# Accumulating weight transfers ordered behind two sums on POOL's queue in a Strassen-style FFN

## The chip, the cores and the metric

The kernel runs on 1 core of one Trainium2 chip. The metric is the device time of one execution in microseconds (us), the median of several runs. The core has five engines that run unsynchronized except for semaphores: PE (matrix multiply), DVE (vector), ACT (activations and copies), POOL (general purpose, and the issuer of transfers that add to their destination) and SP (issuer of plain transfers).

## The reference

Two layers of a decoder trunk over 512 tokens of width 1024, float32. Each layer is four blocks, and the first and the last are gated feed-forward blocks (FFN), so the program holds four of them:

```python
def swiglu(x, w_in, w_out):
    a, b = jnp.split(x @ w_in, 2, axis=-1)
    return (jax.nn.silu(a) * b) @ w_out

for l in range(DEPTH):   # DEPTH = 2; D_MODEL = 1024, D_FF = 2816
    x = layer_norm(ALPHA * x + 0.5 * swiglu(x, ffn1_w_in[l], ffn1_w_out[l]), ...)
    x = layer_norm(ALPHA * x + hybrid_mixer(x, ...), ...)
    x = layer_norm(ALPHA * x + cross_attention(x, mem, ...), ...)
    x = layer_norm(ALPHA * x + 0.5 * swiglu(x, ffn2_w_in[l], ffn2_w_out[l]), ...)
```

## The kernel before, in words

**Arithmetic.** Every float32 operand of a matmul is kept as two rounded parts, high (H) and low (L). A product is three matmuls: `wH` with `xTH`, `wH` with `xTL`, `wL` with `xTH` (printed in this order in the profile as `xTH,wH`, `xTL,wH`, `xTH,wL`). `prep` makes the parts of a weight tile `raw`: ACT copies to `wH`, then DVE writes `wL = raw - wH`. With `share` DVE does only half of `wL` and POOL the other half. The activations x^T lie in `xTH` and `xTL`.

**First half of an FFN.** The columns of `w_in` are worked in 22 column groups of 128 for the gate (part 0) and for the linear factor (part 1). The first four groups (`PLAIN = 2` pairs, f = 0 to 3) are plain products. Groups f = 0, 1 have their first 256 tokens computed while the block before still finishes (`early`, matmuls 256 wide), then their last 256 tokens, and f = 2, 3 run over all 512 tokens (matmuls 512 wide). In the second FFN of layer 0 the four weights of f = 2, 3 are the tiles numbered 7585 (f = 2, part 0), 7616 (f = 2, part 1), 7649 (f = 3, part 0) and 7680 (f = 3, part 1), as `wH`; their `wL` have the next number (7586, 7617, 7650, 7681), and the PSUM banks they fill are 7589, 7620, 7653 and 7684.

The other 9 pairs (q = 2 to 10) use a Strassen-Winograd scheme: 2x2 blocks, seven products instead of eight. It needs four sums and differences of blocks of x^T (T1 to T4) once per FFN, and for each q sums and differences of weight blocks.

**The T's (`combine`).** Four tiles `xr` are xTH + xTL of the four blocks of x^T: POOL makes B11 and B21 (both of the first 256 tokens, `xr_7512` and `xr_7518` in the second FFN), DVE makes B12 and B22 (`xr_7514`, `xr_7516`). DVE then takes differences one from the other, beginning with `xr_7512 <- xr_7514 - xr_7512`, which needs POOL's first sum, and each difference is split into H and L by a copy on ACT and a subtraction on DVE (tiles `T`).

**The weight sum S1.** For each q a tile `sw` is loaded with a plain transfer from SP's queue, and two transfers from POOL's queue then add the second block to it while they write (`accum_op=ALU.add`, two slices of 256 KB each). POOL's queue holds two tiles' worth ahead (`bufs=2`), so two of these pairs stand in POOL's order near the start of an FFN.

**What sets the order.** Nothing in the code fixes POOL's order in general. A scheduler places each engine's instructions by priority and by its own estimate of when operands are ready; each engine then runs its list strictly in that order, and waits at an instruction until its semaphores are reached. `add_manual_dep` with `NoSync` adds an edge that the scheduler must respect, without a semaphore. In the first FFN (program start) the scheduler put POOL's two `xr` sums ahead of the accumulating transfers; in the other three it put two pairs of transfers (four instructions) ahead of the sums.

## Time and profile before

| | us |
|---|---|
| median of 3 runs | 2257.73 (2257.27 to 2258.74) |
| the profiled execution's own time | 2261.62 |
| its span in the trace | 2259.9 |
| PE busy in that span | 2199.5 |
| DVE / ACT / POOL busy | 1449.6 / 928.7 / 287.4 |
| time of PE without an instruction, put down to DVE's `wL` | 38.6, in 8 waits |

Times in the rows are microseconds from the span's start. A timeline row gives the start, the duration, engine, line, operation, `out<-in` without buffer numbers, shapes and count (several like instructions can be merged into one row), and in brackets the engine's idle time before it and the work that ended it. A row of waits gives the waiter, what it waited for, the total, the number of times and the longest.

### The profile page before, as it was taken

What the parts mean: (1) busy time and instruction counts of PE and PEld (TensorE: products, weight loads), DVE (VectorE), ACT (ScalarE), POOL (GpSimd) and SP (SyncE); (2) the same over time, 40 slices, a digit from 0 to 9 for tenths busy, and PEclk for the clock granted to TensorE, in tenths of its full rate; (3) what the DMA queues carried; (4) which work ended last, traced back from release to release, by engine and by line L of the source; (5) the groups of instructions that cost most, each with busy time, mean ns of one, the idle gap of its engine ahead of it and who ended that gap; (6) DMA issues with size and microseconds to landing.
All of it is one profiled execution on the core that took longest, in us unless ns stands there. A gap on an engine that the chain in (4) does not pass through costs nothing.

```text
span 2259.9 us, 33859 instructions
## 1 busy us (share of the span) xinstructions
PE 2199.5 (97%) x13952; PEld 1980.9 (88%) x13952; DVE 1449.6 (64%) x2016; ACT 928.7 (41%) x1405; POOL 287.4 (13%) x336
## 2 busy tenths in 40 slices
PE   9999999999999989999979999999999999899998
PEld 8999888888788879998869998888887988799987
DVE  6677636777675667773457776367776755777734
ACT  4444512467433234461224454134674332344511
POOL 3110001340010211100121100014300102111000
PEclk9999999999999989999989999999999999899999
DMA  8565433223331446643265554232233215456431
GB/s 227 158 166 150 140 103 96 77 86 112 100 112 56 140 112 159 168 150 103 78 170 149 143 147 136 88 114 74 73 112 112 94 56 145 122 145 167 150 103 47
DMA packets 238143, 273.62 MB, mean 121 GB/s; under 512 B 8058, under 2 KB 196762, under 8 KB 237988
## 3 DMA queue, kind: packets, MB, share of 16 engines
q1 hardware_dynamic: 218404, 252.58, 35.1%
q0 software_dynamic: 19584, 18.88, 5.6%
q8 instruction: 109, 1.79, 0.3%
q14 instruction: 46, 0.38, 0.1%
HBM read 267.76 MB, written 3.67 MB: 120 GB/s over the span
## 4 chain that ended last, share of the span: by engine, by line
PE 83%; DVE 8%; issue 4%; POOL 2%; DMA 1%; ACT 1%; SPq 0%; DVEq 0%; POOLq 0%; ACTq 0%
PE ps L194 81%; DVE wL L121 2%; PE ps L199 2%; DVE x_nat L121 1%; DVE xTL L121 1%; DVE st L121 1%; DMA sw<-in_ffn_w_in_dram 1%; POOL mlrs L121 1%; POOL sw L121 1%; DVE xr L121 0%; DVE T L121 0%; POOL xr L121 0%; DVE Cb L121 0%; DMA x_nat<-in_x_dram 0%; DMA raw<-in_ffn_w_in_dram 0%
## 5 line engine op out<-in xcount | busy, mean ns | idle before, releaser
L121 DVE TENSOR_TENSOR wL<-raw,wH 128x1024 fp32r<-128x1024 f32 (+2 forms) x423 | 504.8, 1195 | 488.9 <-ACT wH L121 484.9
L121 ACT CAST wH<-raw 128x1024 fp32r<-128x1024 f32 (+2 forms) x423 | 439.9, 1044 | 767.7 <-PE ps L194 572.7
L194 PE MATMUL ps<-xTH,wL 128*128 128x256 f32 (+1 forms) x1712 | 525.1, 307 | 38.1 <-DVE wL L121 38.1
L194 PE MATMUL ps<-xTH,wH 128*128 128x256 f32 (+1 forms) x1712 | 527.5, 309 | 1.0 <-ACT sc L121 1.0
L194 PE MATMUL ps<-xTL,wH 128*128 128x256 f32 (+1 forms) x1712 | 525.1, 307 | 2.9 <-DVE xTL L121 2.9
L194 PE MATMUL ps<-T,wH 128*128 128x256 f32 x2304 | 418.6, 283 | 0.0
L194 PEld LDWEIGHTS ps<-xTH,wL 128*128 128x128 f32 x1712 | 330.0, 193 | 55.2 <-DVE wL L121 40.8
L194 PEld LDWEIGHTS ps<-T,wH 128*128 128x128 f32 x2304 | 359.4, 192 | 0.5
L194 PEld LDWEIGHTS ps<-xTL,wH 128*128 128x128 f32 x1712 | 330.2, 193 | 17.9 <-DVE xTL L121 5.3
L194 PEld LDWEIGHTS ps<-xTH,wH 128*128 128x128 f32 x1712 | 329.9, 193 | 14.5 <-ACT sc L121 1.2
L194 PE MATMUL ps<-T,wL 128*128 128x256 f32 x1152 | 326.3, 283 | 0.5 <-DVE wL L121 0.5
L194 PE MATMUL ps<-wH,hH 128*128 128x512 f32 x704 | 274.6, 390 | 0.0
L194 PE MATMUL ps<-wH,hL 128*128 128x512 f32 x704 | 274.5, 390 | 0.0
L194 PE MATMUL ps<-wL,hH 128*128 128x512 f32 x704 | 274.1, 389 | 0.0
L194 PEld LDWEIGHTS ps<-T,wL 128*128 128x128 f32 x1152 | 221.2, 192 | 0.9 <-DVE wL L121 0.7
L121 POOL DMA_DIRECT2D sw<-in_ffn_w_in_dram x72 | 87.7, 1219 | 627.0 <-issue 245.9
L121 POOL TENSOR_TENSOR rs<-ve,mhalf 128x1 f32<-128x1 f32 x32 | 29.8, 931 | 1079.0 <-DVE ve L121 1079.0
L194 PEld LDWEIGHTS ps<-wH,hL 128*128 128x128 f32 x704 | 132.1, 188 | 28.4 <-DVE hL L121 1.3
L194 PEld LDWEIGHTS ps<-wL,hH 128*128 128x128 f32 x704 | 132.2, 188 | 27.3
L194 PEld LDWEIGHTS ps<-wH,hH 128*128 128x128 f32 x704 | 132.2, 188 | 27.2
L121 ACT CAST wH<-sw 128x1024 fp32r<-128x1024 f32 x72 | 75.5, 1048 | 130.9 <-DVE sw L121 90.7
L121 DVE TENSOR_TENSOR wL<-sw,wH 128x1024 fp32r<-128x1024 f32 x72 | 87.9, 1221 | 22.6 <-ACT wH L121 22.5
(243 smaller groups left out, 2964.6 us busy)
## 6 DMA issues: line engine op xcount, KB each, us to landing
raw<-in_ffn_w_in_dram SPq DMA_DIRECT2D x147, 512.0 KB, 6.2
raw<-in_ffn_w_out_dram SPq DMA_DIRECT2D x40, 1024.0 KB, 5.0
raw<-in_ffn_w_in_dram SPq DMA_DIRECT2D x28, 1024.0 KB, 7.1
sw<-in_ffn_w_in_dram SPq DMA_DIRECT2D x36, 512.0 KB, 3.5
sw<-in_ffn_w_in_dram POOLq DMA_DIRECT2D x72, 256.0 KB, 4.6
raw<-in_xattn_w_kv_dram SPq DMA_DIRECT2D x16, 1024.0 KB, 5.6
raw<-in_mix_w_in_dram SPq DMA_DIRECT2D x18, 512.0 KB, 4.0
raw<-in_mix_w_in_dram SPq DMA_DIRECT2D x8, 1024.0 KB, 5.2
```

Of the source, the lines that this page charges most:

```text
L121: return f(*a, **k)
L194: self.nc.tensor.matmul(out, l, r, start=start, stop=stop, **k)
L199: self.nc.tensor.transpose(out, i, ident)
```

## The change

The transfers that add to `sw` get an edge behind POOL's second sum (`self.summed`, the last instruction that the loop over the four sums made, which is B21 on POOL). The edge is order alone, on one engine; no wait is added. The helper that made such edges for `behind` is split out as `order`.

```diff
     def behind(self, ins, i):
 
         if self.hold is not None:
-            self.tc.add_manual_dep(ins.ins, self.hold[i].ins.name, mybir.DependencyInfo(
-                mybir.DependencyClass.NoSync, mybir.DependencyReason.DATA), reason="order")
+            self.order(ins, self.hold[i])
+
+    def order(self, ins, before):
+        self.tc.add_manual_dep(ins.ins, before.ins.name, mybir.DependencyInfo(
+            mybir.DependencyClass.NoSync, mybir.DependencyReason.DATA), reason="order")
...
         for e, x in ((G, "B11"), (V, "B12"), (V, "B22"), (G, "B21")):
             H, L = self.right(x)
             r[x] = self.two("xr").rearrange("p a (k n) -> p (a k) n", k=2)
-            e.tensor_add(r[x], H.bitcast(F32), L.bitcast(F32))
+            i = e.tensor_add(r[x], H.bitcast(F32), L.bitcast(F32))
+        self.summed = i
...
             for k in (0, 2):
-                nc.gpsimd.dma_start(s[:, k:k + 2], self.block(q, 1, 1)[:, k:k + 2], accum_op=ALU.add)
+                i = nc.gpsimd.dma_start(s[:, k:k + 2], self.block(q, 1, 1)[:, k:k + 2], accum_op=ALU.add)
+
+                n.order(i, self.summed)
```

The number of instructions on each engine is the same. The order differs at one place of the second, third and fourth FFN, and there in the same way; the first FFN keeps its order.

POOL, at the start of the second FFN's transfers (`sw_7717` and `sw_7882` are the S1 tiles of q = 2 and q = 3):

```order
 L121 TENSOR_TENSOR wL_7416<-raw_7413,wH_7415 128x512
+L121 TENSOR_TENSOR xr_7512<-xTH_7114,xTL_7115 128x1024
+L121 TENSOR_TENSOR xr_7518<-xTH_7114,xTL_7115 128x1024
 L121 DMA sw_7717<-in_ffn_w_in_dram 128x2x256 x2
 L121 DMA sw_7882<-in_ffn_w_in_dram 128x2x256 x2
-L121 TENSOR_TENSOR xr_7512<-xTH_7114,xTL_7115 128x1024
-L121 TENSOR_TENSOR xr_7518<-xTH_7114,xTL_7115 128x1024
 L121 DMA sw_8107<-in_ffn_w_in_dram 128x2x256 x2
```

The two sums moved up past four accumulating transfers. DVE, at the same place (`h_7461` is the gated hidden tile of f = 0, multiplied by its second factor in bank 7342):

```order
+L121 TENSOR_TENSOR xr_7514<-xTH_7114,xTL_7115 128x1024
+L121 TENSOR_TENSOR xr_7516<-xTH_7114,xTL_7115 128x1024
+L121 TENSOR_TENSOR h_7461<-h_7461,ps_7342 128x512
+L121 TENSOR_TENSOR xr_7512<-xr_7514,xr_7512 128x1024
 L121 TENSOR_TENSOR wL_7586<-raw_7583,wH_7585 128x1024
-L121 TENSOR_TENSOR xr_7514<-xTH_7114,xTL_7115 128x1024
-L121 TENSOR_TENSOR h_7461<-h_7461,ps_7342 128x512
-L121 TENSOR_TENSOR xr_7516<-xTH_7114,xTL_7115 128x1024
-L121 TENSOR_TENSOR xr_7512<-xr_7514,xr_7512 128x1024
-L121 TENSOR_TENSOR wL_7617<-raw_7614,wH_7616 128x1024
 L121 TENSOR_TENSOR xr_7514<-xr_7516,xr_7514 128x1024
```

The first weight's `wL_7586` now stands behind the difference that needs POOL's sum, and `wL_7617` left this place. It turns up further down DVE's list, behind the last T:

```order
 L121 TENSOR_TENSOR h_7461<-h_7461,ps_7420 128x512
 L121 TENSOR_TENSOR T_7460<-xr_7518,T_7459 128x1024
+L121 TENSOR_TENSOR wL_7617<-raw_7614,wH_7616 128x1024
 L121 TENSOR_TENSOR wL_7650<-raw_7647,wH_7649 128x1024
 L121 TENSOR_TENSOR wL_7681<-raw_7678,wH_7680 128x1024
 L121 TENSOR_TENSOR wL_7723<-raw_7711,wH_7722 128x1024
```

On ACT, the copies `T_7455`, `wH_7680` and `T_7459` now follow each other in this order; `T_7460` above needs `T_7459`. PE, at the second 512-wide product:

```order
 L194 MATMUL ps_7620<-xTH_7114,wH_7616 128x512
 L194 MATMUL ps_7620<-xTL_7115,wH_7616 128x512
+L194 MATMUL ps_7653<-xTH_7114,wH_7649 128x512
+L194 MATMUL ps_7653<-xTL_7115,wH_7649 128x512
+L194 MATMUL ps_7684<-xTH_7114,wH_7680 128x512
+L194 MATMUL ps_7684<-xTL_7115,wH_7680 128x512
 L194 MATMUL ps_7620<-xTH_7114,wL_7617 128x512
```

Four matmuls that need no `wL` moved ahead of the first one that needs `wL_7617`, so 30 of the 512-wide matmuls stand ahead of it, and 26 before.

## The prediction

> **What bounds the kernel now.** I read the busy times first, then who PE waits for, then PE's rows around its longest waits, then backwards from there.

> ```profile
> PE 2199.5 (97%) x13952; PEld 1980.9 (88%) x13952; DVE 1449.6 (64%) x2016; ACT 928.7 (41%) x1405; POOL 287.4 (13%) x336
> PE ps L194 <- DVE wL L121: 38.6, 8, 11.5
> ```

> PE is the bound. It has few idle microseconds, and 38.6 of them are waits for a low weight half (`wL`), up to 11.5 at a time. So a change off PE can gain about this much, with what follows from the waits. PE's rows show where they lie, in FFNs two, three and four:

> ```profile
> 787.37 0.40 PE L194 MATMUL ps<-xTH,wH 128*128 128x512 f32 x1
> ...
> 793.07 0.39 PE L194 MATMUL ps<-xTL,wH 128*128 128x512 f32 x1
> 803.26 0.79 PE L194 MATMUL ps<-xTH,wL 128*128 128x512 f32 x1 [9.81 <-DVE wL L121]
> ...
> 812.94 0.50 PE L194 MATMUL ps<-xTH,wL 128*128 128x512 f32 x1 [1.06 <-DVE wL L121]
> ...
> 1169.64 0.80 PE L194 MATMUL ps<-xTH,wL 128*128 128x512 f32 x1 [11.47 <-DVE wL L121]
> ...
> 1179.32 0.50 PE L194 MATMUL ps<-xTH,wL 128*128 128x512 f32 x1 [1.60 <-DVE wL L121]
> ...
> 1928.72 0.79 PE L194 MATMUL ps<-xTH,wL 128*128 128x512 f32 x1 [11.46 <-DVE wL L121]
> ...
> 1938.40 0.50 PE L194 MATMUL ps<-xTH,wL 128*128 128x512 f32 x1 [2.18 <-DVE wL L121]
> ```

> In each, PE starts the 512-wide products, stops after 26 matmuls at the first that needs `wL_7617`, and stops again 24 matmuls later at `wL_7650`. From 787.37 to 793.07 are 25 steps, 0.228 each. After the long wait the step is longer, since the granted clock is down:

> ```profile
> 803.26:809.40 6.14, 6.13 (x14) 0.50 0.51 171
> 1938.40:1944.00 5.60, 5.60 (x18) 0.70 0.79 241
> ```

> (stretch, its length, PE busy and count, granted clock, DMA share, GB/s). So a long wait costs its length and some 4 us at half clock behind it. Why `wL_7617` is late, from POOL's and DVE's rows:

> ```profile
> 768.48 1.70 POOL L121 TENSOR_TENSOR wL<-raw,wH 128x512 fp32r<-128x512 f32 x1 [1.03 <-ACT wH L121]
> 779.43 1.30 POOL L121 DMA_DIRECT2D sw<-in_ffn_w_in_dram  x1 [9.25 <-PE ps L194]
> 784.15 1.22 POOL L121 DMA_DIRECT2D sw<-in_ffn_w_in_dram  x1 [3.43 <-issue]
> ...
> 795.86 5.12 POOL L121 TENSOR_TENSOR xr<-xTH,xTL 128x1024 f32<-128x1024 f32 x2
> 798.73 3.35 DVE L121 TENSOR_TENSOR xr<-xr,xr 128x1024 f32<-128x1024 f32 x1 [14.70 <-POOL xr L121]
> 802.00 1.21 DVE L121 TENSOR_TENSOR wL<-raw,wH 128x1024 fp32r<-128x1024 f32 x1
> ```

> POOL is free at 770.18, waits 9.25 for its first accumulating transfer's turn, issues four over 16 us, and only then makes its sums. DVE waits 14.70 for the first sum, with `wL_7617` behind that wait; PE starts 0.05 after `wL_7617` ends.

> **The change, part by part.** *What the stalls cost.* Without stalls the matmul of 803.26 starts one step after 793.07, at 793.30: lost 9.96 (the bracket's 9.81, plus the 0.16 by which a matmul's 0.39 outlasts a step). The 24 steps to 812.94 take 9.68 instead of 5.47: 4.2 more, the half clock and the second wait. In sum 14.2. In the third FFN likewise 11.47 + 0.16 + (9.68 - 5.47) = 15.8, in the fourth 11.46 + 0.16 + 4.21 = 15.8. There the clock drops once more: 18 matmuls start in 5.60, 17 steps, 3.9 at 0.228: 1.7. Sum: 47.5.

> *What takes their place.* POOL's sums can start at 770.18 in place of the wait: both read the first 256 tokens only, whose x^T stood before the early products used it. The first FFN has exactly the new order of POOL, DVE and ACT there, and so shows the new chain's lengths:

> ```profile
> 25.94 5.74 POOL L121 TENSOR_TENSOR xr<-xTH,xTL 128x1024 f32<-128x1024 f32 x2
> 31.61 1.37 POOL L121 DMA_DIRECT2D sw<-in_ffn_w_in_dram  x1
> 36.57 1.23 POOL L121 DMA_DIRECT2D sw<-in_ffn_w_in_dram  x1 [3.59 <-issue]
> 26.83 5.94 DVE L121 TENSOR_TENSOR xr<-xTH,xTL 128x1024 f32<-128x1024 f32 x2
> 32.69 0.68 DVE L121 TENSOR_TENSOR h<-h,ps 128x512 f32<-128x512 f32 x1
> 34.42 1.21 DVE L121 TENSOR_TENSOR wL<-raw,wH 128x1024 fp32r<-128x1024 f32 x1
> 44.30 2.35 DVE L121 TENSOR_TENSOR wL<-raw,wH 128x1024 fp32r<-128x1024 f32 x2
> 35.70 0.37 SPq L251 DMA_DIRECT2D raw<-in_ffn_w_in_dram  x1
> 41.03 1.05 ACT L121 CAST wH<-raw 128x1024 fp32r<-128x1024 f32 x1 [0.91 <-DMA raw<-in_ffn_w_in_dram]
> ```

> POOL: 770.2 + 5.7 = 775.9 for both sums. DVE's own two sums end within 1.1 of that (there 26.83 + 5.94 = 32.77 against 31.68), 777.0. The product on `h` needs the bank 7342, done 48 matmuls 256 wide (0.12 each, 5.8) before 787.37, so it starts at about 781.9: DVE's sums are hidden with 4 us to spare. `wL_7586`, now behind it and the difference, ends (34.42 + 1.21 - 32.69 =) 2.9 after `h` starts, 784.8; PE needs it at 787.37 + 2 x 0.228 = 787.8. Hidden by 3 us; if the sums were late, it would not be.

> `wL_7617` is the new end of a chain: `wL_7586` frees its raw buffer, SP then loads the last raw tile (7678), ACT casts it and, queued behind that, `T_7459`; DVE makes `T_7460` and then `wL_7617`. In the first FFN the load took 41.03 - 35.70 = 5.3 from issue, and from there to the end of the first of two `wL` (44.30 + 1.2) are 4.5. Here: issue 784.9, then 5.3 and 4.5, 794.7. PE needs it at 787.37 + 30 x 0.228 = 794.2 with its four matmuls moved ahead. The six loads of this size from 741 to 782 bound it, in the view of the raw tiles:

> ```profile
> DMA to landing us min/median/max: 5.2/6.0/6.9
> ```

> With 5.2 the wait is 0.4, with 6.9 it is 2.1. I take the median, 6.0: 1.2 a time, 3.6 in three. Behind it `wL_7650` and `wL_7681` follow every 1.14 while PE has 22 matmuls (5 us) before each: hidden.

> *A collision.* POOL's first sum now meets DVE's half of `wL_7416`:

> ```profile
> 770.02 0.36 PE L194 MATMUL ps<-xTH,wH 128*128 128x256 f32 x1
> 770.15 0.68 DVE L121 TENSOR_TENSOR wL<-raw,wH 128x512 fp32r<-128x512 f32 x1
> 770.75 1.28 DVE L121 TENSOR_TENSOR xTL<-ps,xTH 128x512 fp32r<-128x512 f32 x2
> ```

> Two such operations did not run together above: DVE's 798.73 took 3.35 instead of 1.21 beside POOL's second sum, and in the first FFN they took turns. DVE would lose one POOL operation, about 2.4, and end at 773.2; PE needs this `wL` 26 matmuls after 770.02, at 773.1. Cost 0 to 0.3 a time; I take 0.1, 0.3 in all. `xTL` then ends near 774.5, needed 48 matmuls after 770.02, at 775.8: hidden.

> *The moved transfers.* They stay where the load of `sw` lets them start: the 9.25 wait at 779.43 names PE, yet in the third FFN the same wait ends on the load of `sw`:

> ```profile
> 1145.16 1.25 POOL L121 DMA_DIRECT2D sw<-in_ffn_w_in_dram  x1 [10.26 <-DMA sw<-in_ffn_w_in_dram]
> ```

> POOL is through its sums by 775.9, so nothing moves. Then the first S1 tile is complete about 5 after 784.15, at 789; PE reads its product after 96 matmuls 512 wide and 24 of 256, 787.37 + 21.9 + 2.9 = 812. Cover some 20 us. `wH` of the second S1 tile comes a whole q later.

> *Sum.* 47.5 - 3.6 - 0.3 = 43.6. The profiled execution, 2261.62 (span 2259.9), would come to 2218.0; the median of the runs is 3.9 below the profiled one, and from 2257.73 I get 2214.1, so 2214. Bounds: no remaining wait, 2210; all waits 2.1 and collisions 0.3, 47.5 - 7.2 = 40.3, 2217.

> A wait may also cost clock. Those of 1.06 and 1.60 were followed by full steps, that of 2.18 by the 1.7 us of loss in the row from 1938.40. With it in all three: 40.3 - 5.1 = 35.2, 2222 to 2223. [...]

> **Rivals.** *The stall shrinks to the last load.* If the load of 7678 shares the engines with the accumulating transfers for longer, everything behind it slides. Against it: the first FFN had the same company and took 5.3. For it: the transfers to `sw` have landed as late as the third figure here.

> ```profile
> DMA to landing us min/median/max: 4.1/4.6/9.0
> ```

> At 9.0 the wait is 4.2, with 1.7 to 4.2 of clock behind it: 5.9 to 8.4 a time, 18 to 25 in three, 2228 to 2236. *Slower: the first weight is caught too.* If POOL's sums ended after 785.4, DVE's difference (1.1) and `wL_7586` (1.2) would miss 787.8. Were they as late as before (difference done at 802.1), PE would stop 24 matmuls earlier than now, 5.5 us, and find `wL_7617` eight or nine DVE operations of 1.14 behind: about 7 more a time, 2257.7 + 21 = 2279. It needs POOL held until 780. The load of `sw` no longer stands ahead of the sums; and if PE, which the row at 779.43 names, held them as well, they would end at 779.4 + 5.7 = 785.1, just in time. Late S1 transfers give the same sign only if they land after 812. Could DVE, now busy while POOL issues, hold the issues up? In the first FFN, with DVE busy, two issues were 36.57 - 31.61 = 4.96 apart; here, with DVE idle, 784.15 - 779.43 = 4.72. So 0.24 is lost per issue, against 20 us of cover: no time. [...] *No change*: the new place of `wL_7617` costs 14 us, as the old. It would have to end near 808, a load of 19 us; nothing is near.

> **How the numbers follow.** Forecast, 2208 to 2222: 0.86. Last load late, 2222 to 2240: 0.08. No change: 0.02. Slower: 0.04. A measurement of this kernel can tell about 0.2%, 4.5 us, from no change. Faster 0.94, same 0.02, slower 0.04. The range is the forecast's with the near end of the first rival, 2208 to 2224; its low end leaves 2 us below the stall-free bound for the runs' own spread.

> **What would show it.** POOL's two sums directly behind its last `wL`, ahead of 780; DVE's `h` and first difference back to back at 782; no wait of PE over 2.2 on `wL`, three of 0.4 to 2.1; no half clock of more than 2 us behind them; the wait total for `wL` from 38.6 to under 7; transfers to `sw` at the same offsets. Wrong if ACT's cast of 7678 waits long for its load, if PE waits for `wL_7586`, or if a wait appears later in the Strassen loop that starts 14 us earlier.

## The result, and the profile after

The three runs of the changed kernel took 2219.27, 2221.45 and 2224.46 us, median 2221.45, against 2257.73 before: ratio 0.984, 95% interval 0.9817 to 0.9862. Five more runs gave 2221.52 (2217.44 to 2222.98). The prediction said 2214, range 2208 to 2224. It was right in sign, place and mechanism; the gain is 36.3 us in the medians where 43.6 was forecast. The profiled execution took 2221.45 (span 2219.7).

The busy times, then the view of waits (waiter, what it waited for, us in all, times, longest):

```profile
PE 2191.3 (99%) x13952; PEld 1975.3 (89%) x13952; DVE 1454.1 (66%) x2016; ACT 929.3 (42%) x1405; POOL 291.1 (13%) x336
```

```profile
PE ps L194 <- DVE wL L121: 5.4, 4, 2.6
PE ps L199 <- DVE x_nat L121: 3.0, 5, 1.0
```

The waits for `wL` fell from 38.6 to 5.4. PE's rows at the same places (the first 512-wide product of the second FFN, then every wait on `wL` in FFNs two to four; the third FFN starts 12 us and the fourth 27 us earlier than before):

```profile
786.79 0.40 PE L194 MATMUL ps<-xTH,wH 128*128 128x512 f32 x1
...
795.31 0.50 PE L194 MATMUL ps<-xTH,wL 128*128 128x512 f32 x1 [1.53 <-DVE wL L121]
...
1147.68 0.50 PE L194 MATMUL ps<-xTH,wL 128*128 128x512 f32 x1 [0.49 <-DVE wL L121]
...
1893.90 0.79 PE L194 MATMUL ps<-xTH,wL 128*128 128x512 f32 x1 [2.61 <-DVE wL L121]
```

The 9.81, 11.47 and 11.46 have become 1.53, 0.49 and 2.61, and the second waits are gone. Only the last is followed by a slow step (0.79). In the view of stretches (length, PE busy, granted clock, DMA share, GB/s):

```profile
1893.00:1905.00 12.00, 11.10 (x42) 0.86 0.92 274
```

A clock of 0.86 over 12 us is 3.4 us at half clock (it reads 0.50 from 1893.63 to 1897.03), 1.7 us lost. Around the second FFN's stall, POOL, DVE, SP's queue and ACT now read:

```profile
769.55 6.31 POOL L121 TENSOR_TENSOR xr<-xTH,xTL 128x1024 f32<-128x1024 f32 x2
778.70 1.30 POOL L121 DMA_DIRECT2D sw<-in_ffn_w_in_dram  x1 [2.84 <-DMA sw<-in_ffn_w_in_dram]
783.44 1.22 POOL L121 DMA_DIRECT2D sw<-in_ffn_w_in_dram  x1 [3.45 <-issue]
781.30 0.69 DVE L121 TENSOR_TENSOR h<-h,ps 128x512 f32<-128x512 f32 x1 [4.36 <-ACT h L121]
781.90 1.22 DVE L121 TENSOR_TENSOR xr<-xr,xr 128x1024 f32<-128x1024 f32 x1
783.04 1.22 DVE L121 TENSOR_TENSOR wL<-raw,wH 128x1024 fp32r<-128x1024 f32 x1
792.89 1.22 DVE L121 TENSOR_TENSOR T<-xr,T 128x1024 fp32r<-128x1024 f32 x1 [1.23 <-ACT T L121]
794.04 3.49 DVE L121 TENSOR_TENSOR wL<-raw,wH 128x1024 fp32r<-128x1024 f32 x3
784.32 0.37 SPq L251 DMA_DIRECT2D raw<-in_ffn_w_in_dram  x1
790.86 1.05 ACT L121 CAST wH<-raw 128x1024 fp32r<-128x1024 f32 x1 [2.11 <-DMA raw<-in_ffn_w_in_dram]
791.82 1.04 ACT L121 CAST T<-xr 128x1024 fp32r<-128x1024 f32 x1
```

POOL's two sums stand ahead of its transfers, which start at 778.70 on the landing of `sw`, as before (779.43). DVE's difference follows `h` at once. What remains is the chain that the prediction named: `wL_7586` (783.04), the last raw load (784.32, landed 790.86), ACT's two copies, `T_7460` (792.89), `wL_7617`.

### The profile page after: what moved, and what is told of

Its sections match the earlier page's. It is cut to its first block, busy times and chain, and to the rows that moved or that the text cites. A ratio compares the mean times of both kernels' runs of the same rounds, so it can differ in the third digit from the quotient of the medians.

```text
span 2219.7 us, 33854 instructions
## 1 busy us (share of the span) xinstructions
PE 2191.3 (99%) x13952; PEld 1975.3 (89%) x13952; DVE 1454.1 (66%) x2016; ACT 929.3 (42%) x1405; POOL 291.1 (13%) x336
## 4 chain that ended last, share of the span: by engine, by line
PE 86%; DVE 7%; issue 2%; DMA 2%; POOL 1%; ACT 1%; DVEq 0%; SPq 0%; ACTq 0%; POOLq 0%
PE ps L194 84%; DVE wL L121 2%; PE ps L199 2%; DVE x_nat L121 1%; DMA raw<-in_ffn_w_in_dram 1%; DVE st L121 1%; DVE xTL L121 1%; POOL mlrs L121 1%; ACT wH L121 0%; DVE Cb L121 0%; DMA x_nat<-in_x_dram 0%; DMA biasD<-scr 0%; DVE stL L121 0%; DVE mlst L121 0%; DVE hid L121 0%
## 5 line engine op out<-in xcount | busy, mean ns | idle before, releaser
L121 DVE TENSOR_TENSOR wL<-raw,wH 128x1024 fp32r<-128x1024 f32 (+2 forms) x423 | 506.7, 1200 | 477.6 <-ACT wH L121 473.5
L121 ACT CAST wH<-raw 128x1024 fp32r<-128x1024 f32 (+2 forms) x423 | 439.7, 1044 | 785.5 <-PE ps L194 562.4
L194 PE MATMUL ps<-xTH,wL 128*128 128x256 f32 (+1 forms) x1712 | 520.6, 305 | 5.4 <-DVE wL L121 5.4
L194 PE MATMUL ps<-xTH,wH 128*128 128x256 f32 (+1 forms) x1712 | 524.2, 307 | 1.0 <-ACT sc L121 1.0
L194 PE MATMUL ps<-xTL,wH 128*128 128x256 f32 (+1 forms) x1712 | 522.1, 305 | 2.9 <-DVE xTL L121 2.9
L194 PE MATMUL ps<-T,wH 128*128 128x256 f32 x2304 | 418.6, 283 | 0.0
L194 PEld LDWEIGHTS ps<-T,wH 128*128 128x128 f32 x2304 | 359.3, 192 | 0.5
L194 PEld LDWEIGHTS ps<-xTH,wL 128*128 128x128 f32 x1712 | 327.8, 192 | 20.5 <-DVE wL L121 6.9
L194 PEld LDWEIGHTS ps<-xTL,wH 128*128 128x128 f32 x1712 | 328.0, 192 | 17.3 <-DVE xTL L121 5.3
L194 PEld LDWEIGHTS ps<-xTH,wH 128*128 128x128 f32 x1712 | 328.0, 192 | 14.3 <-ACT sc L121 1.2
L194 PE MATMUL ps<-T,wL 128*128 128x256 f32 x1152 | 326.3, 283 | 0.0
L194 PE MATMUL ps<-wH,hH 128*128 128x512 f32 x704 | 274.5, 390 | 0.0
L194 PE MATMUL ps<-wH,hL 128*128 128x512 f32 x704 | 274.4, 390 | 0.0
L194 PE MATMUL ps<-wL,hH 128*128 128x512 f32 x704 | 273.9, 389 | 0.0
L194 PEld LDWEIGHTS ps<-T,wL 128*128 128x128 f32 x1152 | 221.1, 192 | 0.2
L121 POOL TENSOR_TENSOR rs<-ve,mhalf 128x1 f32<-128x1 f32 x32 | 30.1, 940 | 1081.2 <-DVE ve L121 1081.2
L121 POOL DMA_DIRECT2D sw<-in_ffn_w_in_dram x72 | 87.8, 1219 | 582.1 <-issue 242.2
L194 PEld LDWEIGHTS ps<-wH,hL 128*128 128x128 f32 x704 | 132.1, 188 | 28.7 <-DVE hL L121 1.3
L194 PEld LDWEIGHTS ps<-wL,hH 128*128 128x128 f32 x704 | 132.2, 188 | 27.3
L194 PEld LDWEIGHTS ps<-wH,hH 128*128 128x128 f32 x704 | 132.2, 188 | 26.8
L121 ACT CAST wH<-sw 128x1024 fp32r<-128x1024 f32 x72 | 75.6, 1050 | 123.2 <-DVE sw L121 94.2
L121 DVE TENSOR_TENSOR wL<-sw,wH 128x1024 fp32r<-128x1024 f32 x72 | 88.0, 1223 | 26.1 <-ACT wH L121 26.1
```

The costliest lines, as they stand in the source:

```text
L121: return f(*a, **k)
L194: self.nc.tensor.matmul(out, l, r, start=start, stop=stop, **k)
```

## The experiments

Theory A: PE waited since DVE's first difference and the `wL` behind it stood behind POOL's queue of transfers; what is left hangs on the last raw load. "Before" is a median of runs on the same chip each time (2257.69 to 2259.05).

**DVE's order without POOL's.** POOL's list of before, and one edge (`wL_7586`, here `n.sub`, behind the first difference) that gives DVE the order of after:

```diff
+        if f == 2 and part == 0 and not self.start:
+            n.order(n.sub, self.diff)
```

> The kernel before with POOL's list as it was (four transfers ahead of the two sums), but DVE's list as in the changed kernel: wL_7586 is ordered behind the first difference. This is the prediction's slower rival made real. Theory A: PE stops after 6 matmuls of 512 (near 788.8) until the difference (802.1) and wL_7586 (803.3) are through, 14.5 us and some 4 of half clock, and again 2 to 5 us at wL_7617, which stands eight or nine DVE operations behind: 20 to 24 us lost in each of three FFNs where the kernel before loses 15: 2270 to 2285, the prediction said 2279. Theory E (the place of wL_7586 in DVE's list does not matter, since PE would wait for wL_7617 until the same moment anyway): 2255 to 2262.

Measured: 2271.54, slower than before by a ratio of 1.0053 (1.0035 to 1.0070). Its view of waits, then two of PE's rows:

```profile
PE ps L194 <- DVE wL L121: 47.8, 7, 15.0
```

```profile
801.09 0.79 PE L194 MATMUL ps<-xTH,wL 128*128 128x512 f32 x1 [14.37 <-DVE wL L121]
...
1182.03 0.61 PE L194 MATMUL ps<-xTH,wL 128*128 128x512 f32 x1 [2.60 <-DVE wL L121]
```

Theory A's 14.5 came as 14.37, 13.67 and 14.97, at the low end of its time because the second waits were 2.60 at most. Theory E falls. The lists of DVE, PE and SP are those of the changed kernel, and ACT's differ by one exchange in each FFN; POOL's order makes most of the 50 us between them. So the edge on POOL is the gain, and DVE's new list without it is a loss.

**All four sums on DVE**, POOL's order of before:

```diff
-        for e, x in ((G, "B11"), (V, "B12"), (V, "B22"), (G, "B21")):
+        for e, x in ((V, "B11"), (V, "B12"), (V, "B22"), (V, "B21")):
```

> The kernel before, without the order edge, but DVE makes all four sums; POOL keeps its transfers where they were and makes no sum. DVE's list has two sums more (2 x 1.2) ahead of the first difference. Theory A (the gain is that the first difference and the weight halves behind it no longer stand behind POOL's queue of transfers; who makes the sums does not matter): as the changed kernel to within some 4 us: the product on h starts at 781.9, two sums and the difference and wL_7586 end at 787, where PE needs wL_7586 at 787.3 to 787.8; wL_7617 then as in the changed kernel or up to 1.5 later: 2219 to 2227. Theory D (the gain comes from the changed place of the transfers on the chip, or from POOL working beside DVE): nearer to the kernel before, over 2240.

Measured: 2239.21, ratio 0.9905 (0.9879 to 0.9932). That is 19.8 below its before, a little over half of the gain: a miss for A's number, and 0.8 short of D's. So the number decides nothing and the rows have to. DVE's rows and SP's queue:

```profile
786.33 0.69 DVE L121 TENSOR_TENSOR h<-h,ps 128x512 f32<-128x512 f32 x1 [7.59 <-ACT h L121]
786.94 2.35 DVE L121 TENSOR_TENSOR xr<-xTH,xTL 128x1024 f32<-128x1024 f32 x2
789.21 1.22 DVE L121 TENSOR_TENSOR xr<-xr,xr 128x1024 f32<-128x1024 f32 x1
790.34 1.22 DVE L121 TENSOR_TENSOR wL<-raw,wH 128x1024 fp32r<-128x1024 f32 x1
791.62 0.37 SPq L251 DMA_DIRECT2D raw<-in_ffn_w_in_dram  x1
```

DVE stood idle for 7.59 us with the two added sums in its list behind `h`. So `wL_7586` came 4.01 after `h` and not 1.74, and the load of 7678 was issued 5.29 after `h`, not 3.02. PE then waited 1.02 to 2.08 for `wH_7680` and 2.61 for `wL_7617` in FFNs two to four (0.89 and 2.29 in the first), with 3.4 or 6.8 us at half clock behind in each FFN. These waits and that clock are what A's number left out.

**The four sums ahead of `h`**, all on DVE (`sums`), with no edge on the transfers, and on ACT `T_7459` ahead of `wH_7680` (the last two lines, which stand earlier in the file, are that edge):

```diff
-            V.tensor_mul(h, h, bs[1])
             if f == 0:
+                self.sums()
+            i = V.tensor_mul(h, h, bs[1])
+            if f == 0:
+                n.order(i, self.summed)
                 self.combine()
...
-                n.order(i, self.summed)
...
+                    if f == 3 and part == 1 and not self.start:
+                        n.order(n.cast, self.t4)
```

> All four sums on DVE, ordered ahead of the product on h, where DVE stands idle for 4 to 8 us; POOL makes no sum, and its transfers need no edge. On ACT the copy T_7459 stands ahead of wH_7680, as in the run with that edge. Theory A (what counted in the run with four sums on DVE was that two of them stood behind h, so that wL_7586, and with it the last raw load, came 2.3 us later): the sums (4.7 us) now lie in DVE's idle time, wL_7586 ends where it does in the changed kernel, no wait of PE on wL over 0.5 in FFN two to four: 2213 (2209 to 2218). Theory F (POOL's early sums met DVE's last normalisation of x_nat and so cost the 1.0 and 2.2 us waits at the third FFN's entry): without sums on POOL no wait for x_nat over 0.6 anywhere and a spread of the runs of some 3 us. Theory G (DVE has no room for the sums): over 2225.

Measured: 2223.85 (2223.29 to 2224.34), ratio 0.9845 (0.9831 to 0.9858). The sums are free here (DVE still idles 5.3 us before `h`) and the load is issued 3.02 after `h`. Yet PE waits 1.66 for `wH_7680` and 0.72 for `wL_7617`, the same in all three FFNs. ACT's rows say why:

```profile
790.53 0.60 ACT L121 ACTIVATE h<-ps 128x512 f32<-128x512 f32 x1 [2.46 <-PE ps L194]
791.03 1.04 ACT L121 CAST T<-xr 128x1024 fp32r<-128x1024 f32 x1
791.96 1.05 ACT L121 CAST wH<-raw 128x1024 fp32r<-128x1024 f32 x1
```

The scheduler put the activation of the next `h`, which waits for PE, ahead of both copies, and the edge held `wH_7680` behind them. Theory A's number missed; the chain ran through ACT's order again, with another head. Theory D falls: POOL makes no sum here and its transfers have no edge, and the gain is there all the same. The longest wait for `x_nat` is 0.5, as F said.

**The edge from the first sum only.**

```diff
-        self.summed = i
+            if x == "B11":
+                self.summed = i
```

> The edge reaches only back to POOL's first sum (B11); the first accumulating transfer then stands between POOL's two sums, and the second sum (B21) comes some 9 us later, near 780, when the load of sw has landed. Theory A (what DVE's list waits for first is the first sum; the second is wanted only at the fourth difference, near 788.7): as the changed kernel within 4 us, 2219 to 2224. Theory H (both sums have to be ahead of all transfers): a stall of DVE at the fourth difference and waits of PE on wL_7617 of several us, over 2228.

Measured: 2228.15 (2225.35 to 2230.43), ratio 0.9863 (0.985 to 0.9877), at the foot of H's range, but not by H's stall: DVE waits for nothing at the fourth difference (788.49). DVE and POOL:

```profile
778.93 2.86 POOL L121 TENSOR_TENSOR xr<-xTH,xTL 128x1024 f32<-128x1024 f32 x1
781.00 1.89 DVE L121 TENSOR_TENSOR xr<-xr,xr 128x1024 f32<-128x1024 f32 x1
```

POOL's late sum met DVE's first difference (1.89, not 1.22), `wL_7586` and the load came 0.7 later after `h`, the load took 7.1 us (784.09 to ACT's copy at 791.23) and not 6.5, and PE's waits on `wL_7617` became 2.61, 2.61 and 2.60, each with half clock. Neither theory had this.

**What remains: ACT's order.** The changed kernel with one more edge (the last two lines of the diff above, alone):

> The changed kernel with one more order edge: on ACT the copy T_7459 (the H half of the fourth T) stands ahead of the copy wH_7680, so that it no longer waits for the load of the last raw tile; DVE, PE, POOL and SP keep their lists. Theory A (the remaining waits of PE on wL_7617 come from that load, through ACT's order): the waits of 1.53, 0.49 and 2.61 us go, and with the last one the half clock behind it (1.7), some 6 us in all: 2215 (2212 to 2219). T_7460 would end near 786 and wL_7617 near 789 in the second FFN, against a need at 793.6. Theory B (DVE or ACT is simply too busy between the first product and wL_7617, whatever the load does): the waits stay within 0.5 us of what they were, 2221. Theory C (the wait moves to wH_7680, whose copy now stands behind T_7459): PE waits on ACT's wH at the first FFN matmuls, 2219 to 2223.

Measured: 2216.14 (2214.72 to 2223.99), ratio 0.9812 (0.9783 to 0.9842). No wait on `wL` over 0.22 is left in FFNs two to four, one of 0.69 on `wH` in the third: A, with a trace of C. The longest of the four runs is the profiled one; it has a 2.50 wait in the first FFN, and this at the third's entry (DVE, POOL, PE):

```profile
1121.62 4.56 DVE L121 SCALAR_TENSOR_TENSOR x_nat<-x_nat,rs,scr 128x512 f32<-128x512 f32 x2
1122.84 5.57 POOL L121 TENSOR_TENSOR xr<-xTH,xTL 128x1024 f32<-128x1024 f32 x2
1126.32 1.09 PE L199 MATMUL ps<-ident,x_nat 128*128 128x128 f32 x4 [2.19 <-DVE x_nat L121]
```

Two operations of DVE that took 1.41 at other entries took 4.56 beside POOL's `wL` half and first sum.

**What remains: the load itself.** Raw tiles kept, so that each is loaded once (the condition is on the family of the key, in `raw`):

```diff
-            self.raws = {k: v for k, v in self.raws.items() if k[0] == key[0]}
+            self.raws = {k: v for k, v in self.raws.items()
+                         if k[0] == key[0] or isinstance(key[0], tuple) and k[0][0] == key[0][0]}
```

> The changed kernel, but the raw tile of a pair of f is kept for its second half while the other part's raw tile is loaded, so that each 1 MB raw tile of the plain products is loaded once and not twice: four loads fewer in each of FFN two, three and four (two fewer in the first). ACT's and DVE's lists move with it. Theory A (the remaining waits hang on the load of raw 7678): with no load behind wL_7586 all three waits go, with the half clock 6 us: 2215 (2211 to 2219). Theory B (DVE too busy): waits stay, 2221. If the lower traffic also ends the 1.0 us wait for x_nat ahead of the third FFN, up to 2 us more.

Measured: 2233.05, ratio 0.9882 (0.9853 to 0.9911), slower than the changed kernel. The waits on `wL` in FFNs two to four are gone, as A said, but waits for `x_nat` have come. The view of waits, then PE, POOL and DVE at the second FFN's entry:

```profile
PE ps L199 <- DVE x_nat L121: 16.0, 10, 2.6
```

```profile
768.49 0.92 PE L199 MATMUL ps<-ident,x_nat 128*128 128x128 f32 x4 [2.58 <-DVE x_nat L121]
771.33 0.88 PE L199 MATMUL ps<-ident,x_nat 128*128 128x128 f32 x3 [1.92 <-DVE x_nat L121]
...
764.51 0.92 POOL L121 TENSOR_TENSOR rs<-ve,mhalf 128x1 f32<-128x1 f32 x1 [0.76 <-DVE ve L121]
765.40 5.24 POOL L121 TENSOR_TENSOR xr<-xTH,xTL 128x1024 f32<-128x1024 f32 x2
765.61 5.58 DVE L121 SCALAR_TENSOR_TENSOR x_nat<-x_nat,rs,scr 128x512 f32<-128x512 f32 x2
```

With the early weights loaded sooner, the scheduler put POOL's last `wL` half ahead of `rs`, and POOL's sums directly behind it, on top of DVE's normalisation: 5.58 in place of 1.41.

**Only the pair f = 2 and 3 kept**, the entry as it was:

```diff
+        name = (self.tag, part) if f < 2 else (self.tag, part, "pair")
...
-            ... if k[0] == key[0]}
+            ... if k[0] == key[0] or len(k[0]) == len(key[0]) == 3 and k[0][0] == key[0][0]}
```

> The changed kernel, with the raw tiles kept only for the pair f = 2 and 3 (two loads of 1 MB fewer in each FFN, the last one of 7678 among them), and the early products loaded as before, so that DVE's and POOL's lists at the entry of an FFN stay as they are. Theory A with F (in the run that kept all raw tiles the waits on wL were gone, and what made it slower was POOL's sums and a weight half that moved into DVE's normalisation at the entry): no wait on wL in FFN two to four, no two waits of 2 us for x_nat in FFN two and four: 2215 (2211 to 2219), up to 2224 in runs in which POOL's sum still meets the normalisation ahead of the third FFN. Rival (the kept raw tiles themselves are at fault, by buffers that come free later): 2228 or more, with waits on wH or wL in the Strassen loop.

Measured: 2213.91 (2212.88 to 2215.42), ratio 0.9801 (0.9787 to 0.9814). One wait on `wL` of 0.84 is left in FFNs two to four, and no half clock between the program's start and its end. A and F together hold, the rival falls: what made the run before slow was the entry. POOL's list is that of the changed kernel, but the scheduler ordered PE, DVE and ACT differently too with the two loads gone, so that what the loads alone are worth is not separated from that.

> Four sums on DVE ahead of the product on h, none on POOL, and raw tiles kept for the pair f = 2 and 3; ACT's order is left to the scheduler. Both causes of what is left in the changed kernel are taken away. Theories A and F: no wait on wL and none over 0.6 for x_nat: 2212 (2208 to 2217), the least of all. If it is not below the two runs that take away one cause each, the two overlap.

This is that kernel with the sums on DVE ahead of `h` (the two diffs together, without the edge on ACT). Measured: 2215.99 (2215.53 to 2217.87), ratio 0.9811 (0.9798 to 0.9825): not the least. No wait for `x_nat` over 0.6, as F said, but PE waits 0.87 and 0.65 in the first FFN and 0.80 and 0.67 on `wL` in the third and fourth: by these waits, what the move of the sums saves at the entry it costs elsewhere.

**Both versions side by side.**

> The changed kernel once more, with more runs. The three runs gave 2219.27 to 2224.46, the prediction said 2214. If the short waits (1.53, 0.49, 2.61 in the profiled run) and the half clock after those in which over about 1.8 us fall into one window of 3.41 us are all that is left, runs differ by 1.7 us for each half-clock window: 2217 to 2225, median 2221. A median under 2217 would say that the three runs were high by chance and that the prediction's sizes of the waits were right.

> The kernel that keeps the raw tiles of the pair f = 2 and 3, beside the changed kernel on the same chip. Theory A: 2214 (2212 to 2217), 6 to 9 below the changed kernel, since no wait on wL and no half clock is left in FFN two to four.

Measured: 2221.52 (2217.44 to 2222.98), ratio 0.9838 (0.9824 to 0.9852), and 2212.54 (2212.32 to 2215.14), ratio 0.9799 (0.9785 to 0.9814). So this kernel is 9.0 us below the changed one on the same chip, and below before by 44.9 and 45.2 in its two runs where the changed kernel gained 36.3 and 36.2: 8 to 9 us more. The 1.8 us of the first expectation is the author's estimate from the profiles (in that of before, half clock followed a stretch of 3.41 us with 2.18 of it without a matmul, and full clock one with 1.55), and 3.41 is the shortest stretch at half clock there. The changed kernel's profiled run (2217.44) has no wait at the third FFN's entry, so that this one varies from run to run.

**The transfers late.** In the changed kernel POOL reads one column of the last T ahead of its transfers (the lists of the other engines stay the same):

```diff
+        hold = self.summed
+        if not self.start:
...
+            hold = nc.gpsimd.tensor_copy(tiny, self.T[3][1][:, 0, :1].bitcast(F32))
...
-                n.order(i, self.summed)
+                n.order(i, hold)
```

> The changed kernel, but POOL reads one column of the last T (T_7460, near 794.1 in the second FFN) ahead of its accumulating transfers, in FFN two to four: the first four transfers come some 15 us later, and the load of raw 7678 has no accumulating transfers beside it. The prediction gave the S1 transfers 20 us of cover. If that holds, PE still waits for nothing that comes from sw (first needed by PE at 813.3, ready by some 806). Theory K (the company of the accumulating transfers makes the last load slow, 6.5 us in the profiled run instead of 5.3 in the first FFN): the load takes some 5.3, the waits on wL_7617 fall to 0.5 or less each, no half clock: 2215 to 2218. Theory L (the load's time is its own): the waits stay, 2219 to 2224. If the cover is less than the prediction said: waits of PE on ACT wH or DVE wL of sw near 813, several us in each FFN, over 2230.

Measured: 2228.55 (2225.63 to 2229.27), ratio 0.9865 (0.9851 to 0.988). SP's queue, ACT and PE:

```profile
784.15 0.37 SPq L251 DMA_DIRECT2D raw<-in_ffn_w_in_dram  x1
789.38 1.05 ACT L121 CAST wH<-raw 128x1024 fp32r<-128x1024 f32 x1 [0.80 <-DMA raw<-in_ffn_w_in_dram]
809.28 1.05 ACT L121 CAST wH<-sw 128x1024 fp32r<-128x1024 f32 x1 [10.05 <-DMA sw<-in_ffn_w_in_dram]
816.33 0.39 PE L194 MATMUL ps<-T,wL 128*128 128x256 f32 x1 [0.76 <-DVE wL L121]
...
823.96 0.50 PE L194 MATMUL ps<-T,wH 128*128 128x256 f32 x2 [1.86 <-ACT scr L121]
```

The last load took 5.2, 5.1 and 6.5 us without company, against 6.5, 5.5 and 7.6 in the changed kernel, and the waits on `wL_7617` fell to 0.23 and 0.22 in two FFNs (1.51 in the fourth). Theory K holds for 0.4 to 1.3 us of the load, not for all of the fourth FFN's. The first S1 tile landed at 809.1 (second issue at 801.73, 7.4 to landing), against 788.4 in the changed kernel (783.44 and 5.0), and cost PE 0.76 and, further down DVE's late list, 1.86 in the second FFN: this is the edge of the cover, and past it the time is given back. So neither K's time came nor the 2230 of too little cover.

## Why the prediction was right, point by point

*The bound and the place.* Held. Between PE's first 512-wide products the stretch from the second FFN to the third shrank by 11.3, the next by 15.0, the last by 13.3; the rest of the span moved by 0.6.

*POOL's sums first, DVE after them.* Held: the sums ran from 769.55 to 775.86 (forecast 770.2 to 775.9), `h` at 781.30 (781.9), `wL_7586` done at 784.26 (784.8). The edge on POOL is what did it (2271.54 without it).

*The collision at `wL_7416`.* Forecast 0.3 in all; it cost nothing. DVE's half took 0.68 in the second and fourth FFN (769.57, 1867.06). In the third it did meet POOL's first sum, 1.68 at 1123.44, and PE did not wait for it. A dearer one appeared where the prediction did not look, a few us earlier at this same entry. Rows of PE, DVE and POOL:

```profile
1122.47 0.63 PE L199 MATMUL ps<-ident,x_nat 128*128 128x128 f32 x4 [1.01 <-DVE x_nat L121]
1119.89 2.43 DVE L121 SCALAR_TENSOR_TENSOR x_nat<-x_nat,rs,scr 128x512 f32<-128x512 f32 x2
1123.44 1.68 DVE L121 TENSOR_TENSOR wL<-raw,wH 128x512 fp32r<-128x512 f32 x1
1119.99 1.78 POOL L121 TENSOR_TENSOR wL<-raw,wH 128x512 fp32r<-128x512 f32 x1 [0.27 <-ACT wH L121]
1121.73 5.66 POOL L121 TENSOR_TENSOR xr<-xTH,xTL 128x1024 f32<-128x1024 f32 x2
```

What DVE's 2.43 (1.41 at other entries) met is POOL's `wL` half, not yet a sum. The kernel with POOL's list of before and late sums has it too (2.48 there, PE's wait 0.72), so the edge does not cause it. Theory F in its first form, that the sums made the 1.0 us wait, falls; that early sums make it worse when POOL is through sooner is shown by the 4.56 and 5.58.

*The new end of the chain.* Right chain, size a little off: loads of 6.5, 5.5 and 7.6 for a forecast 6.0 (5.2 to 6.9), waits of 1.53, 0.49 and 2.61 for 1.2 each (0.4 to 2.1): 5.1 with the 0.16 of each, for 3.6. The fourth FFN's load and wait lie outside the bounds. These were thin: only two of the six loads behind 5.2, 6.0 and 6.9 have a landing in the profile, at 5.2 and 6.9. Taking away the load, or ACT's order, took away the waits (0.84 at most was left).

*Clock behind short waits.* The sum's forecast of none was mis-sized: 1.7 us in the profiled run. Two of the signs failed with it: a wait of 2.61 came where none was to pass 2.2, and 3.4 us at half clock behind it, where none of more than 2 was to be. The rows around such waits are below.

*The transfers.* They did not move, and the cover of 20 us was right to within what the late run can tell. POOL's issues show no sign here that DVE's work holds them up, but the prediction's comparison does not tell it: between the two issues before that stand 4.72 apart DVE was not idle, but at work from 779.93 to 784.03. With DVE idle, from there to 798.73, the next two gaps were 6.38 and 4.58; in the changed kernel, with DVE at work nearly all the time from 781.30, the gaps are 4.74, 5.31 and 4.96.

*The sum.* From one profiled execution to the other 40.2 were gained for 43.6: 1.5 of waits, 1.7 of clock and 1.0 at the third entry, less 0.3 and 0.6, are 3.3 of the 3.4. The step that failed is the last one: "the median of the runs is 3.9 below the profiled one" was carried over to a kernel whose profiled run lies on its median (2221.45) or 4.1 below it (2217.44). An excess of one execution is not a constant of the kernel; where it lay in the profile of before no run here shows. The measured 2221.45 is above the 2217 of all waits without clock. It lies in the range by the room left for clock in all three FFNs (5.1), of which 1.7 came; the third entry and the 3.9 used up the rest, and that they fitted in is luck.

## What to carry to other kernels

An instruction that waits for a transfer's turn delays everything behind it on its engine: here a wait of 9.25 us and four issues on POOL kept its sums until 795.86, and DVE waited 14.70 for the first. An edge of order alone, past work whose operands stood ready, was worth 36.3 us (1.6%), and the lists of the engines that follow have to fit it (DVE's new list without POOL's: 2271.54). After such an edge, look for the next chain in the in-order lists (here a load behind a released buffer, and a copy queued behind that load): a transfer not made twice, with the lists that the scheduler then made, was worth another 8 to 9 us. Work moved into DVE's idle time was hidden where it stood ahead of what DVE waits for (5.3 us of idle time left before `h`; 2223.85, with an edge on ACT) and not behind it (7.59 us idle; 2239.21).

## What the runs showed of the hardware

In these runs a wait's length alone did not tell its price: with the four sums ahead of `h`, the same two waits (1.66 and 0.72) were followed by 6.8 us at half clock in the second FFN, none in the third and 3.4 in the fourth, and with the late transfers a wait of 1.86 (before 823.96) was followed by none. The second run of the changed kernel waited 1.90 in its second FFN, over two stretches of 3.41 us, and 1.84 in its fourth, inside one; the view of three such stretches at each place, counted from the half clock at 1891.08:

```profile
788.57:791.99 3.42, 2.97 (x14) 1.00 0.44 56
791.99:795.40 3.41, 1.96 (x9) 1.00 0.33 66
795.40:798.81 3.41, 3.41 (x17) 1.00 1.02 294
1887.67:1891.08 3.41, 1.57 (x7) 1.00 0.63 92
1891.08:1894.49 3.41, 3.41 (x10) 0.50 0.95 313
1894.49:1897.90 3.41, 3.41 (x16) 1.00 1.02 281
```

Behind the stretch with PE busy for 1.96 us (1.45 without a matmul) the clock reads 1.00, behind that with 1.57 (1.84 without) 0.50. What sets the clock these rows do not show, nor where between 1.55 and 1.84 us the change lies.

Sums on DVE took longer beside sums on POOL: DVE's two took 5.58 beside POOL's two (changed kernel, 771.36) and 2.35 where POOL made none (786.94, all sums on DVE). With nearly the same lead the outcome differed: at the third entry POOL's two `wL` halves began 1.29 us ahead of a `wL` of DVE before and 1.28 after, and that one took 0.68 before and 1.82 after. What stood behind it differed too: the two normalisations of `x_nat` took 1.41 before, 2.43 in the changed kernel and 4.56 with the edge on ACT, whose lists on DVE and POOL are the same as the changed kernel's.
